# One mixed encoder layer on one core: the first head's keys move beside the gates' stage, and a weight unit's two parts share a tile

## Chip, core, metric

The kernel runs on one core of a Trainium2 chip. Its time is the device time of one execution in microseconds (us); the number quoted is the median of several runs. The profile is one further execution, recorded by the hardware profiler. The engines are named as in the profile: PE (matrix multiply; PEld its weight loads), DVE (vector), ACT (scalar), POOL, and SP, which here only issues DMAs.

## What is computed

One layer of an encoder, applied to a prompt of 1024 tokens and a sample of 2048, each with 16 learned meta tokens in front; width 1024, all in float32.

```python
xn = _rmsnorm(h, g_pre)
proj = xn @ w_in + b_in
na_q, na_k, na_v, na_z, ml_qk, ml_v, ml_z, ml_o, ml_g, mg = jnp.split(proj, SPLIT_IDX, axis=-1)
ya = (neighbourhood_attention(na_q, na_k, na_v, na_rpb) * silu(na_z)) @ w_a
yb = (mlstm(ml_qk, ml_v, ml_g, ml_o, ...) * silu(ml_z)) @ w_b
ga, gb = jnp.split(jax.nn.sigmoid(mg), 2, axis=-1)
return h + _rmsnorm((ga * ya + gb * yb) @ w_out, g_post)
```

The change touches the mLSTM branch and the weights. In the branch, queries and keys pass a convolution over three tokens and a SiLU; four heads of width 128 then run a gated linear attention in both directions, by chunks: a state per chunk from the keys and values (weighted by the gates), a scan over the states, and outputs from queries, keys, states and decay. The gates come from 16 columns of the projection, by a log-sigmoid, sums and running maxima.

## The kernel before, in words

**Precision.** Every large matmul is done with operands split in two: a high part (ACT copies with rounding) and a low part (DVE subtracts). `mm3` (L199 to L204) makes three products: high by high (L202), low by high (L203), high by low (L204). The names `whi`, `wlo` and `xh`, `xl` are such pairs.

**Two streams in one written order.** `run` (L2080) interleaves two generators. `dense` makes the projections (`group`, `sgates`) and the final stage (`final`) in the order of `PLAN`; `sparse` makes the mLSTM (`ml`) and the attention (`na`) in the order of `STEPS`: mLSTM of the prompt (s = 0), attention of it, mLSTM of the sample (s = 1), attention of it. Each `yield` of `sparse` gives a cost in us, and `dense` is advanced until it has made as much matmul work. So PE's order is written out by hand. The instructions of the other engines, and the DMA issues on SP, are put in order by a scheduler that simulates the program; each engine then works through its own list in order, and an instruction that waits holds all behind it. A tile can be written again when the last reader of its former use is done; pools that are opened later take the memory of pools that are closed.

**Weights.** `wload` (L266) loads a raw unit (128 x 1024 floats) when it is first needed; `wpump` (L277) splits it into `whi` and `wlo` (L303, L304), two tiles with four buffers each, and puts the two stores of the parts into DRAM tensors `wh` and `wl` on a list, `hold`, that `wflush` (L328, L331) empties. When the unit is needed again, two DMAs bring the parts back (L296). Units of key `"q"` are operands for a scheme with seven products in place of eight (`sgates`); there the two tiles hold two prepared operands, each with its own high and low half, loaded from the DRAM tensors `qd` (L289) and read one after the other, 12 matmuls each (L971 to L973). `wtake` hands units to the matmuls, and `wdone` frees them.

**The mLSTM.** `ml` (L1433) opens a pool `keep` for what lives through the whole sequence and, in it, a pool of scratch for `ml_gates` (L1288). That stage makes the decay factors with small matmuls (L1326 to L1394) and leaves them in `keep`. The scratch pool is closed, and a pool for the heads is opened in its place. For each head, `ml_states` (L1480) goes through the blocks of 256 tokens from the last to the first, with the 16 meta tokens as the last item: `load` brings the keys (`raw`, L1416) and the values (`va`, L1476); `conv_a` and `conv_b` make the convolution with its tanh (`cv` L1425 and L1428, `th` L1430) and the finished keys (`kf`, L1503), which are stored for later (L1505); `vsplit` weights and splits the values (`vwh` L1519, `vwl` L1520); PE transposes the keys (L1539), these are split (`kth` L1542, `ktl` L1543), and `mm3` makes the state. `raw`, `va` and `kf` have two buffers each, `cv` and `th` one. `ml_outputs` (L1574) then uses the same tiles for the queries.

**Around it.** While the prompt's mLSTM starts, `dense` is in the second group of the prompt's projections; side work (`tprep`, `wprep`, `nprep`) prepares operands of the seven-product scheme on DVE, ACT and POOL (`po`, `pr`, `xr`).

Of the kernel before, what the change touches and what calls it, by code (L numbers as in the profile page):

```python
# [137 lines left out]
class K:  # L138
# [138 lines left out]
    def wpump(self, most=NBW, parts=1, copy=None):  # L277


        nc, wp = self.nc, self.wp  # L280
        self.wload()
        while self.wraw and self.wout < most:
            key, raw, nk, w = self.wraw.popleft()
            n = nk * w
            hi = wp.tile([P, 4 * WU], F32R, name="whi", bufs=NBW)
            lo = wp.tile([P, 4 * WU], F32R, name="wlo", bufs=NBW)
            if key[0] == "q":
                for x, k in zip((hi, lo), key[1:]):
                    nc.sync.dma_start(x[:, :n].bitcast(F32), self.qd[k][:, :])  # L289
                self.wrdy.append([x[:, :n].rearrange("p (h k c) -> p h k c", h=2, k=4) for x in (hi, lo)])  # L290
                self.wout += 1
                self.wload()
                continue
            if raw is None:
                for x, d in zip((hi, lo), self.wkept[key]):
                    nc.sync.dma_start(x[:, :n].bitcast(F32), d[:, :])  # L296
            else:
                for a in range(parts):
                    c = slice(a * n // parts, (a + 1) * n // parts)
                    if copy:  # L300
                        copy(hi[:, c], raw[:, c])
                    else:
                        nc.scalar.activation(hi[:, c], raw[:, c], AF.Copy)  # L303
                    nc.vector.tensor_tensor(lo[:, c], raw[:, c], hi[:, c].bitcast(F32), op=ALU.subtract)  # L304
                if key[1] in N_COLS and key[0] == "i":
                    j = N_COLS.index(key[1])
                    for a in range(2):
                        d = self.qd[j // 2, f"{j % 2 + 1}{a + 1}"] = self.dp.tile([P, D], F32, name=f"q{j}{a}")
                        for h, x in enumerate((hi, lo)):
                            self.hold.append((d[:, 512 * h:512 * h + 512], x[:, 512 * a:512 * a + 512].bitcast(F32)))  # L310
                else:
                    self.wkept[key] = []
                for x, part in ((hi, "h"), (lo, "l")) if key in self.wkept else ():
                    d = self.dp.tile([P, n], F32, name=f"w{part}{len(self.wkept)}")
                    self.hold.append((d, x[:, :n].bitcast(F32)))
                    self.wkept[key].append(d)
                if not self.early:
                    self.wflush()
                if key[0] in "mo":
                    self.wrdy.append(None)  # L320
                    self.wout += 1
                    self.wload()
                    continue
            self.wrdy.append([x[:, :n].rearrange("p (k c) -> p k c", k=nk) for x in (hi, lo)])
            self.wout += 1
            self.wload()

    def wflush(self, most=99):  # L328
        for _ in range(min(most, len(self.hold))):
            d, x = self.hold.popleft()  # L330
            self.nc.sync.dma_start(d[:, :], x)  # L331

    def wtake(self, n):
        self.wpump()
# [1068 lines left out]
            yield A_G  # L1403
        res += out

    def conv_load(self, mp, src, c0, n, T):

        nc = self.nc
        L = NM + T
        raw = mp.tile([P, BL + 2], F32, name="raw", bufs=2)  # L1410
        a, b = max(c0 - 1, 0), min(c0 + n + 1, L)
        if a > c0 - 1:
            nc.gpsimd.memset(raw[:, 0:1], 0.0)
        if b < c0 + n + 1:
            nc.gpsimd.memset(raw[:, n + 1:n + 2], 0.0)
        nc.sync.dma_start(raw[:, a - c0 + 1:b - c0 + 1], src[:, a:b])  # L1416
        return raw

    def conv(self, mp, raw, h, is_k, n):

        nc = self.nc
        w0 = (12 if is_k else 0) + 3 * h
        w = [self.cw[:, w0 + j:w0 + j + 1] for j in range(3)]
        c = mp.tile([P, BL], F32, name="cv", bufs=1)
        nc.scalar.activation(c[:, :n], raw[:, 0:n], AF.Copy, scale=w[0])  # L1425
        yield
        for j in (1, 2):
            nc.vector.scalar_tensor_tensor(c[:, :n], raw[:, j:j + n], w[j], c[:, :n], op0=ALU.mult, op1=ALU.add)  # L1428
        th = mp.tile([P, BL], F32, name="th", bufs=1)
        nc.scalar.activation(th[:, :n], c[:, :n], AF.Tanh, scale=0.5 / (S_K if is_k else 0.5))  # L1430
        yield th, c

    def ml(self, s):  # L1433
        tc, nc = self.tc, self.nc
        T, self.seq = SEQLEN[s], s
        NB = T // BL
        with tc.tile_pool(name=f"mg{s}", bufs=1, side="right", reuse_waits="tile") as keep:
            with tc.tile_pool(name=f"mt{s}", bufs=1, side="right", reuse_waits="tile") as mp:
                self.tri = mp.tile([P, 2, P], F32, name="tri")
                nc.sync.dma_start(self.tri, self.i["tri"])  # L1440
                self.trim = keep.tile([P, 2, 1, P], F32, name="trim")
                nc.sync.dma_start(self.trim[:, :, 0, :], self.i["trimask"])
                g = []
                yield from self.ml_gates(s, keep, mp, g)
            with tc.tile_pool(name=f"ml{s}", bufs=1, side="right", reuse_waits="tile") as mp:
                self.vas = [mp.tile([P, CB, 130], F32, name=f"va{j}") for j in range(2)]
                for va in self.vas:
                    nc.gpsimd.memset(va[:, :, 128:129], 1.0)
                    nc.gpsimd.memset(va[:, :, 129:130], 0.0)
                norms = deque()  # L1450

                def step():
# [19 lines left out]
    def vload(self, mp, s, h, tok, np_, nch):  # L1472
        nc = self.nc
        va = self.vas[0]
        self.vas = self.vas[1:] + [va]
# [4 lines left out]
    def ml_states(self, mp, s, h, g, NB, sts):  # L1480

        nc = self.nc
# [4 lines left out]
        def load(i):  # L1487
            if i < N:
                n, c0 = seq[i]
                raws[i] = self.conv_load(mp, self.MK[s][h], c0, n, SEQLEN[s])  # L1490
                vas[i] = self.vload(mp, s, h, c0, min(n, P), max(1, n // P))

        def conv_a(i):
            if i < N:
                convs[i] = self.conv(mp, raws.pop(i), h, True, seq[i][0])
                next(convs[i])

        def conv_b(i):
            if i < N:
                n, c0 = seq[i]  # L1500
                th, c = next(convs.pop(i))
                kf = mp.tile([P, BL], F32, name="kf", bufs=2)
                nc.vector.scalar_tensor_tensor(kf[:, :n], th[:, :n], 1.0, c[:, :n], op0=ALU.add, op1=ALU.mult)  # L1503
                if c0:
                    nc.sync.dma_start(self.KF[s][h][:, c0 - NM:c0 - NM + n], kf[:, :n])  # L1505
# [68 lines left out]
    def ml_outputs(self, mp, s, h, g, NB, sts, norms):  # L1574
# [5 lines left out]
        def load(b):  # L1580
            if b < NB:
                t0 = b * BL
                raws[b] = self.conv_load(mp, self.MQ[s][h], NM + t0, BL, SEQLEN[s])
                kfs[b] = kf = mp.tile([P, BL], F32, name="kf", bufs=2)
# [8 lines left out]

        def vnext(b):
            if b < NB:
                vas[b] = self.vload(mp, s, h, NM + b * BL, P, CB)

        def gates(b):

# [5 lines left out]

        def conv_a(b):
            if b < NB:
                convs[b] = self.conv(mp, raws.pop(b), h, False, BL)
                next(convs[b])

        def conv_b(b):
# [51 lines left out]
        def scores(b):  # L1663
# [6 lines left out]
            s1 = mp.tile([P, CB, P], F32, name="s1", tag="th", bufs=1)  # L1670
            nc.scalar.activation(s1, s0[:, :, 1], AF.Copy)
            shs[b] = s0, s1

# [489 lines left out]
```

## Time and profile before

| what | value |
|---|---|
| median of 3 runs | 2701.97 us (2700.68 to 2704.45) |
| the profiled execution | 2708.68 us |
| its span, first to last instruction | 2706.9 us |
| PE busy | 2645.3 us |
| DVE busy | 1941.2 us |
| ACT busy | 1442.0 us |
| DMA | 805.75 MB, mean 298 GB/s |
| mean granted TensorE clock | 0.991 |

A row of a timeline gives the start in us, the length, the engine, the line of the kernel, the operation with out<-in by the program's tile names, and how many such instructions are merged (x2); in brackets stands how long the engine had been idle before it, and who ended that. Lengths of matmuls overlap, since they are pipelined. A row of the waits gives the sum in us, the number of times and the longest. A row of the table by stretches gives the length, the busy time and instructions of PE, PEld, DVE, ACT and POOL, the granted clock (1.00 is full), the busy share of the DMA engines and GB/s.

### The profile page before, as it was taken

To read this page: it belongs to the slowest core of one execution; us is meant where nothing else is said; L and a number is where in the kernel's file an instruction comes from. 1 tells how busy PE (TensorE), PEld (TensorE's weight loads), DVE (VectorE), ACT (ScalarE), POOL (GpSimd) and SP (SyncE) were. 2 spreads that over 40 slices of the span, in tenths; PEclk is the share of its full clock that TensorE was granted. 3 is DMA by queue.
4 is the path that set the end of the run, shared out by engine and by line. 5 is a ranking of instruction groups with operands and counts; after the bars stand their busy time and mean duration, and the time that the engine had idled before them with its cause. 6 is when DMAs were issued, how large, how long until landed. Compare 5 with 4: busy or idle time off the path is not lost.

```text
span 2706.9 us, 47551 instructions
## 1 busy us (share of the span) xinstructions
PE 2645.3 (98%) x15928; PEld 2334.8 (86%) x15928; DVE 1941.2 (72%) x5266; ACT 1442.0 (53%) x3388; POOL 140.0 (5%) x322
## 2 busy tenths in 40 slices
PE   9999799998989999999999999999999999999998
PEld 7998698898977999887888888888889998989888
DVE  5655588778766888545687776867478989897954
ACT  5423456545444655555665566656465665656521
POOL 0112110001000122000000000000000000000000
PEclk9999899999999999999999999999999999999999
DMA  9899887899978899888889998899899898998975
GB/s 368 339 323 341 307 307 240 297 343 339 321 231 280 296 326 313 276 265 271 253 268 328 376 296 274 274 331 362 267 312 311 264 313 270 287 301 264 317 245 208
DMA packets 402052, 805.75 MB, mean 298 GB/s; under 512 B 51632, under 2 KB 180608, under 8 KB 399504
## 3 DMA queue, kind: packets, MB, share of 16 engines
q1 hardware_dynamic: 374864, 708.79, 79.0%
q0 software_dynamic: 26944, 93.93, 9.4%
q8 instruction: 126, 2.06, 0.3%
q14 instruction: 118, 0.97, 0.1%
HBM read 548.96 MB, written 253.60 MB: 296 GB/s over the span
## 4 chain that ended last, share of the span: by engine, by line
PE 82%; DMA 10%; DVE 5%; ACT 1%; issue 1%; SPq 0%; DVEq 0%; ACTq 0%
PE pj L202 9%; PE pj L204 9%; PE pj L203 9%; PE pj L971 7%; PE pj L973 7%; PE pj L972 7%; PE pj L776 4%; PE pj L777 4%; PE pj L778 4%; PE pj L1919 3%; PE pj L1918 3%; PE pj L1920 3%; PE sm L1266 3%; PE tr L1251 2%; DMA wlo<-wl 1%
## 5 line engine op out<-in xcount | busy, mean ns | idle before, releaser
L202 PE MATMUL pj<-xh,whi 128*128 128x512 f32 (+1 forms) x896 | 345.5, 386 | 6.4 <-DMA whi<-wh 4.7
L204 PE MATMUL pj<-xh,wlo 128*128 128x512 f32 (+1 forms) x896 | 337.1, 376 | 6.5 <-DMA wlo<-wl 6.2
L203 PE MATMUL pj<-xl,whi 128*128 128x512 f32 (+1 forms) x896 | 337.6, 377 | 0.1
L776 PE MATMUL pj<-whi,xh 128*128 128x256 f32 (+1 forms) x1152 | 330.8, 287 | 6.7 <-DMA whi<-wh 5.9
L777 PE MATMUL pj<-wlo,xh 128*128 128x256 f32 (+1 forms) x1152 | 325.9, 283 | 0.7 <-DMA wlo<-wl 0.7
L778 PE MATMUL pj<-whi,xl 128*128 128x256 f32 (+1 forms) x1152 | 325.6, 283 | 0.0
L776 PEld LDWEIGHTS pj<-whi,xh 128*128 128x128 f32 x1152 | 218.1, 189 | 7.5 <-DMA whi<-wh 6.1
L1918 PE MATMUL pj<-whi,mh 128*128 128x256 f32 x768 | 219.2, 285 | 0.5 <-DMA whi<-wh 0.5
L777 PEld LDWEIGHTS pj<-wlo,xh 128*128 128x128 f32 x1152 | 217.9, 189 | 1.2 <-DMA wlo<-wl 1.0
L778 PEld LDWEIGHTS pj<-whi,xl 128*128 128x128 f32 x1152 | 218.0, 189 | 0.0
L1920 PE MATMUL pj<-whi,mlo 128*128 128x256 f32 x768 | 216.3, 282 | 0.0
L1919 PE MATMUL pj<-wlo,mh 128*128 128x256 f32 x768 | 216.2, 282 | 0.0
L204 PEld LDWEIGHTS pj<-xh,wlo 128*128 128x128 f32 x896 | 170.3, 190 | 39.8 <-DMA wlo<-wl 7.4
L202 PEld LDWEIGHTS pj<-xh,whi 128*128 128x128 f32 x896 | 170.7, 191 | 36.3 <-issue 6.3
L203 PEld LDWEIGHTS pj<-xl,whi 128*128 128x128 f32 x896 | 170.6, 190 | 27.7 <-issue 1.2
L1258 DVE TENSOR_TENSOR pts<-tr,pts 96x384 fp32r<-96x384 f32 (+2 forms) x192 | 118.5, 617 | 57.1 <-ACT pts L1253 55.2
L1253 ACT ACTIVATE pts<-tr 96x384 fp32r<-96x384 f32 (+2 forms) x192 | 103.5, 539 | 101.7 <-PE tr L1251 101.3
L202 PE MATMUL pj<-yh,whi 128*128 128x512 f32 x384 | 154.3, 402 | 0.0
L203 PE MATMUL pj<-yl,whi 128*128 128x512 f32 x384 | 151.1, 394 | 0.7 <-DVE yl L1820 0.7
L204 PE MATMUL pj<-yh,wlo 128*128 128x512 f32 x384 | 151.6, 395 | 0.0
L1918 PEld LDWEIGHTS pj<-whi,mh 128*128 128x128 f32 x768 | 145.0, 189 | 1.5 <-DMA whi<-wh 0.7
L1919 PEld LDWEIGHTS pj<-wlo,mh 128*128 128x128 f32 x768 | 145.1, 189 | 0.8
(399 smaller groups left out, 7088.1 us busy)
## 6 DMA issues: line engine op xcount, KB each, us to landing
whi<-wh SPq DMA_DIRECT2D x136, 512.0 KB
wlo<-wl SPq DMA_DIRECT2D x136, 512.0 KB
whi<-q SPq DMA_DIRECT2D x62, 512.0 KB
wlo<-q SPq DMA_DIRECT2D x50, 512.0 KB
wraw<-wu SPq DMA_DIRECT2D x48, 512.0 KB
gt<-st SPq DMA_DIRECT2D x96, 256.0 KB
tg<-gt SPq DMA_DIRECT2D x96, 256.0 KB
wh<-whi SPq DMA_DIRECT2D x36, 512.0 KB
```

The costliest lines, as they stand in the source:

```text
L202: mm(out, ah, bh, start=start, stop=False)
L203: mm(out, ah, bl, start=False, stop=False)
L204: mm(out, al, bh, start=False, stop=stop)
L776: nc.tensor.matmul(o, xh, wh, start=k == 0, stop=False)
L777: nc.tensor.matmul(o, xh, wl, start=False, stop=False)
L778: nc.tensor.matmul(o, xl, wh, start=False, stop=k == KT - 1)
L971: mm(bank, w[:, 0, k], xh[:, k], start=fresh and k == 0, stop=False, skip_group_check=True)
L972: mm(bank, w[:, 0, k], xl[:, k], start=False, stop=False, skip_group_check=True)
L973: mm(bank, w[:, 1, k], xh[:, k], start=False, stop=k == 3, skip_group_check=True)
L1918: nc.tensor.matmul(o, mh[:, k, xs], wh, start=clear > 0 and k == 0, stop=False)
L1919: nc.tensor.matmul(o, mh[:, k, xs], wl, start=False, stop=False)
L1920: nc.tensor.matmul(o, ml[:, k, xs], wh, start=False, stop=clear < 2 and k == KT - 1)
```

## The change

Two edits are made together.

1. **Keys of the first head.** The tiles `raw`, `va`, `cv`, `th` and `kf` (and `s1`, which shares a tag with `th`) move from the heads' pool to `keep`, so they don't lie in the memory of the gates' scratch. `ml_states` of head 0 is started ahead of `ml_gates`: its first step issues the loads of blocks 0 and 1. After four steps of `ml_gates` (the log-sigmoid is done, the first gate matmul is not yet written) its second step makes `conv_a(0)` and `conv_b(0)`, with the store of `kf`. The rest, from `vsplit(0)` on, comes after the gates as before, and one yield of `2 * A_D + 8.5` stands for the former two. Heads 1 to 3 do as before.
2. **One tile per weight unit.** `whi` and `wlo` become two halves of one tile `whl` with four buffers; the DRAM tensors of the two parts become one. A reload is one DMA in place of two, a store one in place of two, and the two stores per operand for `qd` become one. Units of key `"q"` are still loaded with two DMAs, one for each half.

```diff
-            hi = wp.tile([P, 4 * WU], F32R, name="whi", bufs=NBW)
-            lo = wp.tile([P, 4 * WU], F32R, name="wlo", bufs=NBW)
+            both = wp.tile([P, 2, 4 * WU], F32R, name="whl", bufs=NBW)
+            hi, lo = both[:, 0], both[:, 1]
...
             if raw is None:
-                for x, d in zip((hi, lo), self.wkept[key]):
-                    nc.sync.dma_start(x[:, :n].bitcast(F32), d[:, :])
+                nc.sync.dma_start(both[:, :, :n].bitcast(F32), self.wkept[key])
...
-                        for h, x in enumerate((hi, lo)):
-                            self.hold.append((d[:, 512 * h:512 * h + 512], x[:, 512 * a:512 * a + 512].bitcast(F32)))
+                        self.hold.append((d.rearrange("p (h c) -> p h c", h=2), both[:, :, 512 * a:512 * a + 512].bitcast(F32)))
                 else:
-                    self.wkept[key] = []
-                for x, part in ((hi, "h"), (lo, "l")) if key in self.wkept else ():
-                    d = self.dp.tile([P, n], F32, name=f"w{part}{len(self.wkept)}")
-                    self.hold.append((d, x[:, :n].bitcast(F32)))
-                    self.wkept[key].append(d)
+                    d = self.wkept[key] = self.dp.tile([P, 2, n], F32, name=f"w{len(self.wkept)}")
+                    self.hold.append((d, both[:, :, :n].bitcast(F32)))
...
-        raw = mp.tile([P, BL + 2], F32, name="raw", bufs=2)
+        raw = self.keep.tile([P, BL + 2], F32, name="raw", bufs=2)
...
-        c = mp.tile([P, BL], F32, name="cv", bufs=1)
+        c = self.keep.tile([P, BL], F32, name="cv", bufs=1)
...
-        th = mp.tile([P, BL], F32, name="th", bufs=1)
+        th = self.keep.tile([P, BL], F32, name="th", bufs=1)
...
-                g = []
-                yield from self.ml_gates(s, keep, mp, g)
-            with tc.tile_pool(name=f"ml{s}", bufs=1, side="right", reuse_waits="tile") as mp:
-                self.vas = [mp.tile([P, CB, 130], F32, name=f"va{j}") for j in range(2)]
+                self.vas = [keep.tile([P, CB, 130], F32, name=f"va{j}") for j in range(2)]
                 for va in self.vas:
                     nc.gpsimd.memset(va[:, :, 128:129], 1.0)
                     nc.gpsimd.memset(va[:, :, 129:130], 0.0)
+                g, self.keep, self.mlp, sts = [], keep, None, {}
+                states = self.ml_states(s, 0, g, NB, sts)
+                next(states)
+                for j, cost in enumerate(self.ml_gates(s, keep, mp, g)):
+                    if j == 3:
+                        next(states)
+                    yield cost
+            with tc.tile_pool(name=f"ml{s}", bufs=1, side="right", reuse_waits="tile") as mp:
+                self.mlp = mp
...
                 for h in range(4):
-                    sts = {}
-                    for cost in self.ml_states(mp, s, h, g, NB, sts):
+                    if h:
+                        sts = {}
+                        states = self.ml_states(s, h, g, NB, sts)
+                    else:
+                        yield 2 * A_D + 8.5
+                    for cost in states:
...
-                kf = mp.tile([P, BL], F32, name="kf", bufs=2)
+                kf = self.keep.tile([P, BL], F32, name="kf", bufs=2)
...
         load(0)
         load(1)
-        yield A_D + (0.0 if h else 8.5)
+        yield A_D
         conv_a(0)
-        yield A_D
+        if h:
+            yield A_D
         conv_b(0)
+        if not h:
+            yield
+            mp = self.mlp
         vsplit(0)
         yield A_D
```

More of the change, by code (lines that the diff above doesn't have):

```diff
@@ L330, in wflush @@
             d, x = self.hold.popleft()
-            self.nc.sync.dma_start(d[:, :], x)
+            self.nc.sync.dma_start(d, x)
     def wtake(self, n):
@@ L1404, in ml_gates, with conv_load @@
         res += out
-    def conv_load(self, mp, src, c0, n, T):
+    def conv_load(self, src, c0, n, T):
         nc = self.nc
         L = NM + T
-        raw = mp.tile([P, BL + 2], F32, name="raw", bufs=2)
+        raw = self.keep.tile([P, BL + 2], F32, name="raw", bufs=2)
         a, b = max(c0 - 1, 0), min(c0 + n + 1, L)
@@ L1417, in conv_load, with conv @@
         return raw
-    def conv(self, mp, raw, h, is_k, n):
+    def conv(self, raw, h, is_k, n):
         nc = self.nc
@@ L1470, in ml, with vload @@
         self.seq = None
-    def vload(self, mp, s, h, tok, np_, nch):
+    def vload(self, s, h, tok, np_, nch):
         nc = self.nc
@@ L1478, in vload, with ml_states @@
         return va
-    def ml_states(self, mp, s, h, g, NB, sts):
-        nc = self.nc
+    def ml_states(self, s, h, g, NB, sts):
+        nc, mp = self.nc, self.mlp
         seq = [(BL, NM + b * BL) for b in range(NB - 1, -1, -1)] + [(NM, 0)]
@@ L1489, in load @@
                 n, c0 = seq[i]
-                raws[i] = self.conv_load(mp, self.MK[s][h], c0, n, SEQLEN[s])
-                vas[i] = self.vload(mp, s, h, c0, min(n, P), max(1, n // P))
+                raws[i] = self.conv_load(self.MK[s][h], c0, n, SEQLEN[s])
+                vas[i] = self.vload(s, h, c0, min(n, P), max(1, n // P))
         def conv_a(i):
             if i < N:
-                convs[i] = self.conv(mp, raws.pop(i), h, True, seq[i][0])
+                convs[i] = self.conv(raws.pop(i), h, True, seq[i][0])
                 next(convs[i])
@@ L1582, in load @@
                 t0 = b * BL
-                raws[b] = self.conv_load(mp, self.MQ[s][h], NM + t0, BL, SEQLEN[s])
-                kfs[b] = kf = mp.tile([P, BL], F32, name="kf", bufs=2)
+                raws[b] = self.conv_load(self.MQ[s][h], NM + t0, BL, SEQLEN[s])
+                kfs[b] = kf = self.keep.tile([P, BL], F32, name="kf", bufs=2)
                 nc.sync.dma_start(kf, self.KF[s][h][:, t0:t0 + BL])
@@ L1595, in vnext @@
             if b < NB:
-                vas[b] = self.vload(mp, s, h, NM + b * BL, P, CB)
+                vas[b] = self.vload(s, h, NM + b * BL, P, CB)
         def gates(b):
@@ L1607, in conv_a @@
             if b < NB:
-                convs[b] = self.conv(mp, raws.pop(b), h, False, BL)
+                convs[b] = self.conv(raws.pop(b), h, False, BL)
                 next(convs[b])
@@ L1669, in scores @@
                 nc.tensor.matmul(s0[:, j, 0], kl[:, j], qh[:, j], start=False, stop=True)
-            s1 = mp.tile([P, CB, P], F32, name="s1", tag="th", bufs=1)
+            s1 = self.keep.tile([P, CB, P], F32, name="s1", tag="th", bufs=1)
             nc.scalar.activation(s1, s0[:, :, 1], AF.Copy)
```

## The prediction

> **What bounds the kernel now.** I read the page first, then the waits of PE, then PE's rows where it stood longest, then the engines in those stretches.
>
> ```profile
> span 2706.9 us, 47551 instructions
> PE 2645.3 (98%) x15928; PEld 2334.8 (86%) x15928; DVE 1941.2 (72%) x5266; ACT 1442.0 (53%) x3388; POOL 140.0 (5%) x322
> ```
>
> TensorE is the bound: 2645.3 of 2706.9 us. The change takes no matmul away, so it can only touch the 61.6 us in which PE does nothing, and what those pauses cost afterwards. The waits of PE say for whom it stands (total, times, longest):
>
> ```profile
> PE tr L1539 <- DVE kf L1503: 14.5, 2, 8.9
> PE pj L204 <- DMA wlo<-wl: 6.2, 2, 3.7
> PE pj L776 <- DMA whi<-wh: 5.9, 1, 5.9
> PE pj L202 <- DMA whi<-wh: 4.7, 1, 4.7
> ```
>
> The first row is the largest and belongs to the start of the first mLSTM head: transposes of the convolved keys `kf` (L1539) wait for DVE to finish them (L1503). The other three are loads of split weights. In order of time, with the pause and its releaser in brackets:
>
> ```profile
> 307.77 0.69 PE L1539 MATMUL tr<-ident,kf 128*128 128x128 f32 x2 [8.86 <-DVE kf L1503]
> 328.88 0.69 PE L1539 MATMUL tr<-ident,kf 128*128 128x128 f32 x2 [5.65 <-DVE kf L1503]
> ...
> 638.86 0.58 PE L776 MATMUL pj<-whi,xh 128*128 128x256 f32 x1 [5.86 <-DMA whi<-wh]
> ...
> 757.08 0.77 PE L202 MATMUL pj<-xh,whi 128*128 128x512 f32 x1 [4.69 <-DMA whi<-wh]
> 761.95 0.79 PE L204 MATMUL pj<-xh,wlo 128*128 128x512 f32 x1 [3.68 <-DMA wlo<-wl]
> ...
> 818.78 0.50 PE L204 MATMUL pj<-xh,wlo 128*128 128x512 f32 x1 [2.53 <-DMA wlo<-wl]
> ```
>
> These six pauses are 31.3 us, half of all that PE loses. A pause costs more than itself. The table by stretches shows the granted clock (PEclk) behind it:
>
> ```profile
> 308.20:311.50 3.30, 3.30 (x17) 3.30 (x16) 2.09 (x5) 0.86 (x3) 0.55 (x2) 0.50 1.03 400
> 312.00:316.00 4.00, 4.00 (x36) 4.00 (x35) 1.21 (x4) 0.75 (x3) 0.00 (x0) 1.00 1.02 410
> 329.30:332.00 2.70, 2.70 (x14) 2.70 (x13) 2.51 (x5) 1.42 (x4) 1.35 (x3) 0.50 0.47 150
> 820.30:823.50 3.20, 3.20 (x8) 1.99 (x6) 0.00 (x0) 0.00 (x0) 0.00 (x0) 0.50 1.04 410
> ```
>
> For about 3.4 us after the first pause and 2.8 us after the second PE runs at half clock, though "busy". Half of that is lost: 1.7 + 1.4 = 3.1 us. So the two pauses on `kf` are worth 14.5 + 3.1 = 17.6 us.
>
> [...]
>
> **First part: the keys of head 0.** What makes `kf` late? The queue that issues loads (SP), in order of time:
>
> ```profile
> 230.90 0.41 SPq L703 DMA_DIRECT2D mk<-st  x1
> ...
> 292.28 0.32 SPq L1416 DMA_DIRECT2D raw<-mk  x1
> ...
> 319.35 0.37 SPq L1476 DMA_DIRECT2D va<-mv  x1
> 319.81 0.41 SPq L1416 DMA_DIRECT2D raw<-mk  x1
> ```
>
> Block 0 needs what the store at 230.90 wrote, but its load goes out only at 292.28: its tile lies where the gates' scratch pool lay. Then two engines work through queues that hold other work:
>
> ```profile
> 300.67 0.49 ACT L1425 ACTIVATE cv<-raw,cw 128x256 f32<-128x256 f32 x1
> 301.07 2.44 ACT L1519 ACTIVATE vwh<-va,g_wT 128x130 fp32r<-128x130 f32 x8
> ```
>
> ```profile
> 303.26 0.48 DVE L1428 SCALAR_TENSOR_TENSOR cv<-raw,cw,cv 128x256 f32<-128x256 f32 x1
> 303.66 1.14 DVE L1520 SCALAR_TENSOR_TENSOR vwl<-va,g_wT,vwh 128x130 fp32r<-128x130 f32 x4
> ...
> 305.11 1.14 DVE L1520 SCALAR_TENSOR_TENSOR vwl<-va,g_wT,vwh 128x130 fp32r<-128x130 f32 x4
> 306.17 1.21 DVE L568 TENSOR_TENSOR po<-pr,po 128x1024 fp32r<-128x1024 f32 x1
> 307.31 0.41 DVE L1503 SCALAR_TENSOR_TENSOR kf<-th,cv 128x256 f32<-128x256 f32 x1
> ```
>
> The convolution is two ACT steps (0.49, and the tanh, near the same) and three on DVE (0.48 twice and 0.41): 2.3 us of work that took from 300.67 to 307.7, since weights' and values' splits stand between.
>
> After the change the tiles `raw`, `va`, `cv`, `th`, `kf` lie in the pool that the gates' results live in, beside the scratch, not on it. Four loads (two of keys, two of values) and the memsets on POOL are traced before the gates; the five steps of block 0 and the store of its `kf` before the gates' first matmul. The yields of this stage sum to the same, so PE's written order is unchanged. The cover for the moved steps:
>
> ```profile
> 265.00:282.00 17.00, 16.89 (x81) 11.87 (x80) 11.40 (x43) 8.82 (x20) 5.03 (x14) 1.00 0.71 261
> ```
>
> ```profile
> 265.19 0.53 PE L1326 MATMUL sm<-g_lf,tri 128*128 128x36 f32 x4
> ```
>
> From the store at 230.90 to the gates' matmuls at 265.19 lie 34 us. Estimate: the store lands in about 7 us, the load takes as much again (a wlo load below takes 7.2 us), so `raw` is in by about 246. In the gates' own 17 us DVE is free for 5.6 and ACT for 8.2; 1.4 us on DVE and about 0.9 us on ACT fit. I cost the moved steps at nothing. If that cover failed, they would stand in front of the gates' chain in the two queues, for the 2.3 us of the work itself, or for a load's 7.2 us (rival three). On SP the moved loads pass weight stores and token loads; four issues of 0.3 to 0.4 us each are 1.5 us on a queue that PE does not wait for there.
>
> What is late next? Without the first pause PE is at the transposes at 307.77 - 8.86 = 298.9. The value split (vwh, vwl) is still traced after the gates. In the trace the first state matmuls came 6.4 us behind the transposes:
>
> ```profile
> 314.15 0.28 PE L202 MATMUL sm<-vwh,kth 128*128 128x260 f32 x1
> ```
>
> At full clock that is 6.4 - 1.7 = 4.7 us, so they would be asked for at 303.6, while both splits of the values ended at 306.2. Bounds: 0 if ACT and DVE do them while the gates end (their inputs are then there), 2.6 us if they stay where they are. I take the middle, 1.3 us.
>
> The second pause, for block 2, hangs on the loads at 319.35 and 319.81. They wait for a free `va` and `raw` buffer, hence for block 0's split and convolution, and for their turn on SP. With block 0 convolved some 40 us earlier, `raw` is free before the gates end, and `va` as soon as the values are split. I count the whole pause as gone; what stands against it is rival one. First part: -17.6 + 1.3 = **-16.3 us**. For the second sequence the same edit may take away a small wait near 1270; bounds 0 and, like the first head's pauses with their clock, a few us; I take 0.
>
> **Second part: one tile and one tensor per unit.** Loads of kept weights, their stores, and the stores of operands for the products become one DMA in place of two. The two largest groups that vanish (issue times in ns: least, median, most):
>
> ```profile
> L296 SPq DMA_DIRECT2D wlo<-wl x144: 319/330/1892, 465.8 to 2675.3; - x144
> ...
> L331 SPq DMA_DIRECT2D wl<-wlo x40: 319/404/1330, 27.5 to 1004.3; - x40
> ```
>
> That is 184 issues and 144 x 0.33 + 40 x 0.40 = 64 us on SP, spread over 2700 us; bytes are the same. SP is not the bound, so this alone is worth nothing; it counts where the second part of a pair stood behind other issues:
>
> ```profile
> 751.18 0.44 SPq L296 DMA_DIRECT2D whi<-wh  x1
> ...
> 754.75 0.59 SPq L296 DMA_DIRECT2D wlo<-wl  x1
> ...
> 815.03 0.32 SPq L296 DMA_DIRECT2D whi<-wh  x1
> 816.24 0.32 SPq L296 DMA_DIRECT2D wlo<-wl  x1
> ```
>
> At 757, whi was 5.9 us under way and wlo 7.2 us (754.75 to 761.95). One DMA issued at 751.18 with twice the bytes lands, as an estimate, 0.52 MB at 300 GB/s = 1.75 us after whi did: 758.8, in place of 761.95. Against the two products that PE did in between (about 0.5 us) that saves some 2.6 us. At 818 the gap is 1.21 us, less than the 1.75 us that the longer transfer adds, so I count nothing. At 638 the same kind of pair, nothing either. On the other side each tight pair can lose 1.75 us. Bounds: a gain of 16.8 us if the four weight pauses vanished, a loss of 1.75 us at each load that is just in time today; I take **-3 us**, by the row at 757.
>
> [...]
>
> **Sum.** -16.3 - 3 = -19.3 us on the profiled execution, which took 2708.68 us with its span of 2706.9. The median of the runs is 2701.97; a stall is as long in either, so the forecast is 2701.97 - 19.3 = 2683 us.
>
> **Rivals.**
>
> One: the second pause takes the place of the first. If the loads of block 2 stay at 319 on SP, PE reaches its transposes at 328.88 - 5.65 - 8.86 - 1.7 = 312.7 and still waits until 328.9. For it: those loads came behind weight stores, and the order on SP is laid out by a scheduler ahead of time. Against: buffers are freed far earlier. Only the merge is left: 2702 - 3 = 2699 us.
>
> Two, on the other side: the pair lands as one. A unit's first product now waits for both parts; and where two prepared operands share a tile, the first can't be reloaded until the second has been read, one operand's 12 matmuls later:
>
> ```profile
> 254.88 0.23 PE pj L202
> ```
>
> ```profile
> 1957.93 0.33 SPq L289 DMA_DIRECT2D whi<-q12s  x1
> ```
>
> ```profile
> 1973.22 0.48 PE L971 MATMUL pj<-xh,whi 128*128 128x512 f32 x1
> ```
>
> 12 x 0.23 = 2.8 us later. The load at 1957.93 is first read at 1973.22, 15.3 us on, among the shortest leads of that stage; 12.5 would be left against flights of 6 to 7 us. That speaks against it. A late unit costs 1.75 us plus half clock (1.7 us): 3.5 us. It decides from 7 such units on (24.7 us, the gain and 0.2% more); 10 of them give 2683 + 35 = 2718 us.
>
> Three: the moved convolution does not fit its cover, stands before the gates' chain and holds PE at 265 for a load's 7.2 us, with the clock's 1.7: 2683 + 9 = 2692 us. The change then moves a pause more than it removes it. Against: 34 us of cover.
>
> **How the numbers follow.** Forecast 0.57, rival one 0.18, two 0.18, three 0.07. About 0.2% (5.4 us) is what a measurement of this kernel tells from no change. Faster by more than that (below 2696.6): the forecast, rival three and 0.04 of rival one, 0.68. Within: the rest of rival one, 0.14. Slower: 0.18. The range goes from 2666 (nothing late next and the weight pauses gone as well: 2702 - 17.6 - 16.8 = 2667.6, and some of their half clock) to 2708 (rival one with a few late units) and leaves out rival two. The forecast's own range is 2666 to 2694.
>
> **What would show it.** Right: no pause of PE at L1539 in the first head; `raw<-mk` issued before the gates' matmuls; half clock gone between 299 and 332; gates at the same place. The pair at 757 with one pause in place of two. Wrong: a pause at L1539 for block 2 as long as both now (rival one); new pauses of PE on the merged tile in many places (rival two); a pause at L1326 or behind it (rival three). All engines' orders are laid out anew, so pauses elsewhere may come and go; if these add more than the 19 us, the forecast fails for a reason that no row here shows.

## The result and the profile after

The changed kernel takes 2699.53 us (median of 20 runs, 2695.07 to 2704.11) against 2703.52 us for the kernel before in the same series: ratio 0.9984, 95% interval 0.9977 to 0.9991. It is faster, by 4.3 us, where 19 were forecast. Two further series gave 0.9979 [0.9970, 0.9988] and 0.9984 [0.9975, 0.9994], on the average -4.8 us. Ratios are turned into us below by 2703.

The profiled executions mislead if they are read by themselves: before's (2708.68 us) lay 5 us above its median, after's (2695.33 us) 4 us below its own. So the two traces differ by 13.4 us, the kernels by 4.8. Places and mechanisms are read from traces here, sizes from the series.

The page of after, first lines:

```profile
span 2693.5 us, 47059 instructions
PE 2642.1 (98%) x15928; PEld 2332.7 (87%) x15928; DVE 1942.3 (72%) x5266; ACT 1437.7 (53%) x3388; POOL 139.5 (5%) x322
```

492 instructions are gone, none of them PE's. The start of head 0 in after, from the timeline: the queue of loads (SP), then PE.

```profile
230.82 0.32 SPq L698 DMA_DIRECT2D mk<-st  x1
...
234.94 1.66 SPq L1411 DMA_DIRECT2D raw<-mk  x2
...
250.25 1.19 SPq L1510 DMA_DIRECT2D kf<-kf  x1
```

```profile
300.51 0.38 PE L1548 MATMUL tr<-ident,kf 128*128 128x128 f32 x2
305.11 0.28 PE L202 MATMUL sm<-vwh,kth 128*128 128x260 f32 x1
```

The keys are loaded 57 us earlier (234.94, before 292.28), and both pauses of PE on `kf` are gone: no bracket stands behind the transposes at 300.51. The stretch 290 to 340 us by itself (PE busy and its matmuls, then the other engines, granted clock, DMA share, GB/s), first before, then after:

```profile
290.00:340.00 50.00, 35.49 (x243) 34.02 (x242) 27.89 (x78) 25.46 (x61) 5.29 (x18) 0.83 0.91 320
```

```profile
290.00:340.00 50.00, 50.00 (x325) 45.34 (x324) 34.65 (x88) 29.06 (x69) 3.81 (x15) 1.00 1.00 354
```

PE loses nothing there in place of 14.5, and the granted clock is 1.00 in place of 0.83. What was gained is given back later. The waits of PE in after, and the places in order of time:

```profile
PE pj L202 <- DMA whl<-w: 8.2, 3, 3.5
PE pj L771 <- DMA whl<-w: 7.4, 2, 6.9
PE sm L204 <- DVE ktl L1552: 6.8, 3, 3.2
```

```profile
441.03 0.39 PE L204 MATMUL sm<-vwh,ktl 128*128 128x260 f32 x1 [3.25 <-DVE ktl L1552]
464.10 0.50 PE L202 MATMUL pj<-xh,whl 128*128 128x512 f32 x1 [1.65 <-DMA whl<-w]
629.88 0.58 PE L771 MATMUL pj<-whl,xh 128*128 128x256 f32 x1 [6.93 <-DMA whl<-w]
747.90 0.47 PE L202 MATMUL pj<-xh,whl 128*128 128x512 f32 x1 [3.05 <-DMA whl<-w]
803.98 0.47 PE L202 MATMUL pj<-xh,whl 128*128 128x512 f32 x1 [3.53 <-DMA whl<-w]
```

The largest wait is now that for the merged tile `whl`: 15.6 us, nearly all between 464 and 804 us. The same matmuls of ones (L370, before L375) run at 419.96 in after and at 435.88 in before, 15.9 us apart. The matmul at 747.90 ran at 757.08 in before: 9.2 us of the 15.9 are left. Whether the merge or the keys' edit did that, a single trace can't say.

### The profile page after: what moved, and what is told of

It reads as the page before. It is cut to its first block, busy times and chain, and to the rows that moved or that the text cites. A ratio compares the mean times of both kernels' runs of the same rounds, so it can differ in the third digit from the quotient of the medians.

```text
span 2693.5 us, 47059 instructions
## 1 busy us (share of the span) xinstructions
PE 2642.1 (98%) x15928; PEld 2332.7 (87%) x15928; DVE 1942.3 (72%) x5266; ACT 1437.7 (53%) x3388; POOL 139.5 (5%) x322
## 4 chain that ended last, share of the span: by engine, by line
PE 79%; DMA 11%; DVE 6%; ACT 2%; issue 1%; SPq 0%; POOL 0%; DVEq 0%; ACTq 0%; POOLq 0%
PE pj L202 8%; PE pj L204 8%; PE pj L203 8%; PE pj L966 7%; PE pj L968 7%; PE pj L967 7%; PE pj L771 4%; PE pj L773 4%; PE pj L772 4%; PE pj L1928 3%; PE pj L1927 3%; PE pj L1929 3%; DMA whl<-w 3%; PE sm L1261 3%; PE tr L1246 2%
## 5 line engine op out<-in xcount | busy, mean ns | idle before, releaser
L202 PE MATMUL pj<-xh,whl 128*128 128x512 f32 (+1 forms) x960 | 369.6, 385 | 9.8 <-DMA whl<-w 8.2
L204 PE MATMUL pj<-xh,whl 128*128 128x512 f32 (+1 forms) x960 | 362.0, 377 | 0.3 <-DVE whl L303 0.3
L203 PE MATMUL pj<-xl,whl 128*128 128x512 f32 (+1 forms) x960 | 360.7, 376 | 0.1
L771 PE MATMUL pj<-whl,xh 128*128 128x256 f32 (+1 forms) x1152 | 331.4, 288 | 8.1 <-DMA whl<-w 7.4
L773 PE MATMUL pj<-whl,xl 128*128 128x256 f32 (+1 forms) x1152 | 327.3, 284 | 0.0
L772 PE MATMUL pj<-whl,xh 128*128 128x256 f32 (+1 forms) x1152 | 326.9, 284 | 0.0
L771 PEld LDWEIGHTS pj<-whl,xh 128*128 128x128 f32 x1152 | 219.2, 190 | 9.2 <-DMA whl<-w 7.8
L772 PEld LDWEIGHTS pj<-whl,xh 128*128 128x128 f32 x1152 | 219.1, 190 | 0.2
L1927 PE MATMUL pj<-whl,mh 128*128 128x256 f32 x768 | 218.3, 284 | 0.9 <-DMA whl<-w 0.9
L773 PEld LDWEIGHTS pj<-whl,xl 128*128 128x128 f32 x1152 | 219.1, 190 | 0.0
L202 PEld LDWEIGHTS pj<-xh,whl 128*128 128x128 f32 x960 | 181.4, 189 | 42.5 <-issue 8.3
L1928 PE MATMUL pj<-whl,mh 128*128 128x256 f32 x768 | 216.3, 282 | 0.0
L1929 PE MATMUL pj<-whl,mlo 128*128 128x256 f32 x768 | 215.5, 281 | 0.0
L204 PEld LDWEIGHTS pj<-xh,whl 128*128 128x128 f32 x960 | 181.4, 189 | 35.5 <-DVE whl L303 0.5
L966 PE MATMUL pj<-xh,whl 128*128 128x512 f32 x512 | 206.7, 404 | 1.1 <-ACT pj L983 1.1
L968 PE MATMUL pj<-xh,whl 128*128 128x512 f32 x512 | 202.0, 395 | 0.0
```

What stands on the lines that cost most here:

```text
L202: mm(out, ah, bh, start=start, stop=False)
L203: mm(out, ah, bl, start=False, stop=False)
L204: mm(out, al, bh, start=False, stop=stop)
L771: nc.tensor.matmul(o, xh, wh, start=k == 0, stop=False)
L772: nc.tensor.matmul(o, xh, wl, start=False, stop=False)
L773: nc.tensor.matmul(o, xl, wh, start=False, stop=k == KT - 1)
```

## The experiments

The theory from here on, **M**: the keys' edit brings what was forecast and the merge takes most of it back. Its rivals: **P**, the profiled execution of before had longer pauses than its usual ones, so the keys' edit has less to win; **O**, every engine's order is laid out anew and the scatter of that is the whole difference.

**Each part alone.** `e1_keys` keeps two tiles, two tensors and two DMAs per unit and moves only the keys; `e2_merge` is the kernel before with `whl` alone:

```
e1:  hi = wp.tile([P, 4 * WU], F32R, name="whi", bufs=NBW)   # as before
     lo = wp.tile([P, 4 * WU], F32R, name="wlo", bufs=NBW)
     ...
e2:  both = wp.tile([P, 2, 4 * WU], F32R, name="whl", bufs=NBW)
     ...
     nc.sync.dma_start(both[:, :, :n].bitcast(F32), self.wkept[key])
```

Beside them ran the two kernels themselves once more.

> Only the first edit: head 0's keys beside the gates; weight units stay two tiles. Theory M (the merge takes back what the keys give): 14 to 18 us faster than before, no pause at the first head's transposes. Theory P (the profiled execution of before had longer pauses than its usual ones): 3 to 6 us faster. Theory O (every order is laid out anew and the pauses of PE move elsewhere): anything from 10 us faster to 5 slower, with the pauses at the first head gone and new ones of as much in the groups behind it.

> Only the second edit: one tile and one tensor per weight unit; keys as before. Theory M: 10 to 14 us slower than before. Theory P: within 3 us of before. Theory O: the pauses at the first head's transposes stay (about 14 us in the profile), the other pauses are drawn anew, and the time lies within 8 us of before on either side.

> The kernel before, unchanged, for a second profile. All theories: ratio 1.000 within 0.1%. Theory P: the two pauses at L1539 are together under 8 us in this profile, in place of 14.5. Theories M and O: 13 to 16 us again.

> The changed kernel, unchanged, for a second profile. All theories: 3 to 5 us faster than before. Theory P: its pauses of PE differ from those of the first profile by 5 us and more in sum. Theories M and O: the same pauses at the same places, within 2 us each.

Measured: the keys alone 2689.77 us, ratio 0.9942 [0.9929, 0.9954], -15.7 us; the merge alone 2711.58 us, 1.0020 [1.0010, 1.0030], +5.4 us; before again 1.0009 [1.0000, 1.0018], after again 0.9979. In a later series the keys alone gave 0.9928 [0.9914, 0.9941], -19.5 us; the mean of both is -17.6. So M holds for the keys (it expected 14 to 18 us) and in its direction for the merge: beside the keys that costs 17.6 - 4.8 = 12.8 us by these means, by itself 5.4, where M had expected 10 to 14. The 12.8 is uncertain by some 3 us, since the means go over several series, and the median of before itself moves between 2702.95 and 2707.88 us from one to the other. In the one series that held both, the changed kernel lies 9 to 10 us above the keys alone (medians 2698.95 and 2689.77, ratios 0.9979 and 0.9942). P falls: the keys alone bring their gain, and the second profile of before has 13.5 us of pauses on `kf`. The merge alone, where PE waits in it:

```profile
303.21 0.44 PE L1534 MATMUL tr<-ident,kf 128*128 128x128 f32 x2 [2.52 <-DVE kf L1498]
320.16 0.69 PE L1534 MATMUL tr<-ident,kf 128*128 128x128 f32 x2 [3.18 <-DVE kf L1498]
...
469.50 0.54 PE L202 MATMUL pj<-xh,whl 128*128 128x512 f32 x1 [2.41 <-DMA whl<-w]
602.36 0.39 PE L771 MATMUL pj<-whl,xh 128*128 128x264 f32 x1 [1.07 <-DMA whl<-w]
...
756.02 0.77 PE L202 MATMUL pj<-xh,whl 128*128 128x512 f32 x1 [6.00 <-DMA whl<-w]
817.18 0.77 PE L202 MATMUL pj<-xh,whl 128*128 128x512 f32 x1 [6.87 <-DMA whl<-w]
```

At 756 one pause of 6.00 stands where 4.69 + 3.68 = 8.37 stood before: a gain of 2.4, as the prediction had it. At 817 6.87 us stand for 2.53, and at 469 and 602 pauses are new: +4.3 + 2.4 + 1.1, on weights +5.4 in sum. That this is also the time measured is chance: the pauses on `kf` fell from 14.5 to 5.7 us here (the keys' load goes out at 286.04, 6 us sooner than in before). So the merge costs some 5.4 + 8.8 = 14 us behind them, about as much as beside the keys' edit.

In all the traces PE runs the same matmuls in the same order, so the start of one and the same matmul can be compared between kernels. By that, e2 is 8.3 us ahead of before at 440 us and 3.7 us behind it at the end: 12 us are lost. At the pause of 469 us it loses 4.3, at that of 817 4.6, both with half clock behind the pause (0.55 and 0.50), and 3.6 at a pause of 1.91 us on DVE (`yg`, at 916.13), where before has none; gains and losses elsewhere nearly cancel.

**What in the merge costs.** Three readings: **W**, the pair lands as one, so a product waits for twice the bytes; **S**, the merged store can start only when the low part is split, and the slot is reloaded only after it; **T**, one tile is one buffer, freed when both parts are done with, whatever DMAs move it. O stays in play. Each kernel is the changed one with some DMAs cut in two:

```
x1:  for h in range(2):                        # reload: two halves of the columns
         c = slice(h * n // 2, (h + 1) * n // 2)
         nc.sync.dma_start(both[:, :, c]..., self.wkept[key][:, :, c])
x2:  for x, h in zip((hi, lo), range(2)):      # reload: by part
         nc.sync.dma_start(x[:, :n]..., self.wkept[key][:, h])
x3:  for h in range(2):                        # store: by part
         self.hold.append((d[:, h], both[:, h, :n]...))
                                               # the operands' stores for qd likewise
x5:  x2 and x3 together                        # only tile and tensor are merged
y7:  x1 and x3 together
```

> The changed kernel, but each kept unit is loaded again by two DMAs, one for each half of its columns with both parts; tile, tensor and store stay merged. So far: keys alone 2689.8, whole change 2699.5, so the merge costs about 10 us beside the keys' edit. Theory W (the pair lands as one: the first product waits for twice the bytes of one long transfer): the first half lands as early as the first part did, the weight pauses shrink to those of the keys alone, 2688 to 2692. Theory S (the merged store starts only when the low part is split, so the reload goes out later): the reload is issued at the same time as in the changed kernel, 2696 to 2700. Theory T (one tile holds both parts and comes free only when both have been read and stored): 2697 to 2702, weight pauses as now. Theory O (the laid out order scatters by several us whatever is edited): any of 2690 to 2705, with pauses at other places.

> The changed kernel, but each kept unit is loaded again by two DMAs, one for each part as before the change; tile, tensor and store stay merged. Theory W: 2688 to 2692, as the keys alone, since a product waits for its own part only. Theory S: about 2697 to 2700, the reloads behind the late stores are still late. Theory T: 2697 to 2702, the weight pauses of 420 to 830 us stay near 20 us in sum. Theory O: any of 2690 to 2705.

> The changed kernel, but a split unit is stored by two DMAs, one for each part as before the change; tile, tensor and reload stay merged. Theory W: no change, 2697 to 2701, the reload still lands as one. Theory S: the high part's store starts ahead of the low part's split, the slot is free earlier, 2690 to 2693. Theory T: 2697 to 2702. Theory O: any of 2690 to 2705.

> The changed kernel with loads and stores by part, all DMAs as before the change; only the tile and the tensor are one for both parts. Theories W and S, each or both: 2688 to 2692, as the keys alone. Theory T: the tile alone makes the loss, 2697 to 2702 with the weight pauses of the changed kernel. Theory O: any of 2690 to 2705, with pauses at other places than the changed kernel's.

Then, on one chip with the keys alone:

> The keys' edit alone once more, now on one chip beside the three kernels below: 2688 to 2692 (first time 2689.8, ratio 0.994), pauses on weights' loads between 400 and 930 us near 8 us in sum. It is the mark for what the merge adds.

> Keys' edit with one tile and one tensor per unit, but all its DMAs by part (first time 2692.3, ratio 0.995, beside another series of runs than the keys alone). Theory T (one tile frees both parts together, so the first part's reload goes out at the second part's time): 4 us or more above the keys alone, 2693 to 2697. Theories W and S (the cost lies in the merged transfers): within 2 us of the keys alone, 2688 to 2692.

> The changed kernel with its reload in two column halves and its store in two parts. If long transfers are what the merge costs (W with S): near the version with all DMAs by part, 2690 to 2693. If the halves add nothing to the stores by part: 2692 to 2696. Theory T: 2694 to 2698.

and, to part the reload from the store within one series:

> The changed kernel once more, beside the three below on one chip: ratio 0.998 as before, pauses on weights' loads of 15 to 17 us between 400 and 930 us. It is the mark for the next two.

> Merged store, reload by part. If the merged reload is the larger cost: 4 to 8 us below the changed kernel of this series. If the merged store is: 0 to 3 us below it (the first series gave 1.6 us).

> Merged reload, store by part. If the merged store is the larger cost: 4 to 8 us below the changed kernel of this series (the first series gave 7 us). If the merged reload is: 0 to 3 us below it; its pauses on weights' loads were not shorter, which speaks for this.

| kernel | ratio to before [95%] | us, by 2703 |
|---|---|---|
| changed kernel, three series | 0.9984 [0.9977, 0.9991], 0.9979 [0.9970, 0.9988], 0.9984 [0.9975, 0.9994] | -4.8 mean |
| x2, reload by part | 0.9973 [0.9962, 0.9983], 0.9981 [0.9969, 0.9992] | -7.3, -5.1 |
| x1, reload by halves | 0.9964 [0.9952, 0.9976] | -9.7 |
| x3, store by part | 0.9956 [0.9941, 0.9971], 0.9965 [0.9953, 0.9977] | -11.9, -9.5 |
| x5, both by part | 0.9950 [0.9933, 0.9967], 0.9940 [0.9926, 0.9954] | -13.5, -16.2 |
| y7, halves and store by part | 0.9934 [0.9921, 0.9948] | -17.8 |
| e1, keys alone | 0.9942 [0.9929, 0.9954], 0.9928 [0.9914, 0.9941] | -15.7, -19.5 |

By their times x1, x2 and x3 of the first series (2696.64, 2697.91 and 2692.57 us) lie where S had put them; W by itself had put x1 and x2 at 2688 to 2692. That series held no changed kernel. In the last one, which did, the medians were 2700.18 (changed), 2697.45 (x2) and 2696.14 us (x3). T falls as the main cause: with all DMAs by part the merged tile is 2.2 and 3.2 us behind the keys alone, and the intervals overlap; a rest of that size for the tile is not excluded. Its mechanism is there: in x5's second run the two parts of the unit read at 799 us are issued together (787.03, two in a row), with the keys alone beside it at 783.82 and 787.46. Of W and S neither does it alone. The store by part brings 6 us (-10.7 against -4.8), the reload by part 1.4 (by halves 5, in one series), both by part 10, and y7 is as fast as the keys alone within the noise. These differences too go across series. Where each acts shows in the queue of loads; first the keys alone, then the changed kernel, then x3:

```profile
442.81 0.33 SPq L331 DMA_DIRECT2D wh<-whi  x1
447.29 0.41 SPq L331 DMA_DIRECT2D wl<-wlo  x1
449.76 0.32 SPq L296 DMA_DIRECT2D whi<-wh  x1
```

```profile
446.33 0.54 SPq L326 DMA_DIRECT2D w<-whl  x1
456.79 1.27 SPq L295 DMA_DIRECT2D whl<-w  x2
```

```profile
438.02 0.33 SPq L328 DMA_DIRECT2D w<-whl  x1
446.05 0.77 SPq L328 DMA_DIRECT2D w<-whl  x1
454.27 0.60 SPq L295 DMA_DIRECT2D whl<-w  x1
```

With two stores the high part is on its way before the low part is split, at 438 to 443 us, and reloads begin at 449.76 or 454.27. The merged store waits until 446.33 (in after ACT is done with the high part at 439.52, DVE with the low part at 444.53), and the first reload behind it goes out at 456.79. That is the new pause at 464 (1.65 us; 3.79 in the third run of the changed kernel, 0.96 in that of x3, none with the keys alone). At the other three the merged reload itself goes out late, as the section on the prediction shows. In the last series, x2 and x3:

```profile
PE pj L772 <- DMA whl<-w: 6.6, 1, 6.6
PE pj L202 <- DMA whl<-w: 4.5, 1, 4.5
```

```profile
PE pj L202 <- DMA whl<-w: 12.5, 3, 7.7
PE pj L773 <- DMA whl<-w: 8.8, 2, 8.1
```

With the reload by part the waits sum to 13.1 us between 400 and 930 us (these two and 2.0 on the low parts), with the reload merged to 21.3, in spite of the better time (x2's trace is its slowest run, 8 us above its median). By place: of the same matmuls, x3 starts that of 419.82 in the third run of the changed kernel 1.5 us sooner (418.36), that of 603.75 6.4 us sooner (597.32), and that of 822.37 only 4.0 us sooner (818.39). So the store by part wins in the stretch of the late store, and behind it the merged reload still loses. How W and S share the cost is settled only roughly, because the waits on DVE and ACT in the same stretch differ as well: 12.7 us in x2 and 7.1 in x3. Of this, 3.6 us are waits on `st` that x3 doesn't have; the rest includes `ktl` (longest 3.25 against 2.65 us) and `yg` (1.91 against 1.05). They come with another order on these engines. O has that much: a few us, not the whole.

**Half the bytes.** To see whether landing itself is what PE waits for, the reload brings the high part alone:

```
nc.sync.dma_start(hi[:, :n].bitcast(F32), self.wkept[key][:, 0])
lo = hi
```

> The changed kernel, but a kept unit's reload brings the high part alone, half the bytes, and the products of the low part read the high part: the low parts are left out of the result, every instruction of PE stays. If the landing of the long transfer is the cause (W): the pauses on weights' loads between 400 and 930 us fall from 15 to 17 us to under 5, the time to 2680 to 2688. If the late start of the reload is (T or S): each pause loses at most the 2 us that half the bytes save, 8 to 10 us stay, 2690 to 2695.

Measured 2682.96 us, 0.9906 [0.9892, 0.9921]. Its waits between 400 and 930 us:

```profile
PE sm L204 <- DVE ktl L1553: 6.0, 4, 3.2
PE sm L202 <- ACT kth L1552: 5.9, 2, 5.3
PE pj L202 <- DMA whl<-w: 2.3, 1, 2.3
```

The waits on weights fall to 2.3 us, from 15.6 in the first trace of the changed kernel (17.1 and 19.2 in the other two). The one that stays is the one at 465 us, behind the merged store. So the waits hang on the bytes of the reload, as W says; S or T by itself would have left 8 to 10 us. Whether the single pair's landing does it or the relief of the DMA engines (from 720 to 930 us busy 0.68 at 228 GB/s, in after 0.80 at 273) can't be told apart here, since the bytes of all kept units were halved.

**Smaller still.** The keys alone, with each part reloaded in two column halves:

```
for h in range(2):
    c = slice(h * n // 2, (h + 1) * n // 2)
    for x, d in zip((hi, lo), self.wkept[key]):
        nc.sync.dma_start(x[:, c].bitcast(F32), d[:, c])
```

> The keys' edit alone, two tiles as before, but each part is loaded again in two column halves: four transfers per unit in place of two. If the size of a transfer matters in itself while the DMA engines are full, the step that cost about 10 us one way brings some the other way: 2683 to 2687. If it costs only because a product waits for bytes that it does not need yet and halves are needed almost at once: 2687 to 2691. If more issues on SP are a price: 2690 to 2695.

Measured 2688.25 us, 0.9938 [0.9921, 0.9955]: the same as the keys alone. So neither the transfer's size nor the number of issues shows a price of its own here, within the interval of 4.6 us on either side. The stretch 600 to 930 us, for after (1 MB per reload), the keys alone (512 KB) and this kernel (256 KB):

```profile
600.00:930.00 330.00, 311.35 (x1992) 282.53 (x1993) 239.95 (x632) 163.22 (x360) 34.57 (x66) 0.97 0.86 299
```

```profile
600.00:930.00 330.00, 316.99 (x2073) 287.87 (x2072) 247.01 (x647) 167.76 (x369) 35.74 (x68) 0.99 0.88 305
```

```profile
600.00:930.00 330.00, 319.98 (x2085) 291.62 (x2084) 248.59 (x651) 170.37 (x373) 37.80 (x72) 0.98 0.89 309
```

The DMA engines move 299, 305 and 309 GB/s; the larger transfers are not faster.

The best version is the keys' edit without the merge: 2689.77 and 2688.96 us, below both kernels.

## Why the prediction was wrong

- **The keys' pauses (-17.6): right.** Both are gone with their half clock, the cover for the moved steps held (the `kf` store is out at 250.25, ahead of the gates), and the part alone measured -15.7 and -19.5 against -16.3.
- **Late next (1.3): wrong place.** Where it was placed, nothing is late: the first state matmul follows the transposes after 4.6 us (300.51, 305.11) without a pause. Other pauses grew instead. Waits of the keys alone between 400 and 930 us:

```profile
PE sm L204 <- DVE ktl L1557: 5.0, 6, 1.7
PE pj L776 <- DMA whi<-wh: 4.6, 1, 4.6
PE pj L204 <- DMA wlo<-wl: 2.7, 2, 1.5
PE sm L202 <- ACT kth L1556: 2.6, 1, 2.6
PE pj L375 <- ACT st L367: 2.2, 1, 2.2
PE pj L777 <- DMA wlo<-wl: 0.8, 1, 0.8
```

- The waits on DVE and ACT are 10 us there (with one of 0.6), 3.4 in before (`ktl` 2.5, `stT` 0.9); those on weights fell from 17.5 (6.2 + 5.9 + 4.7 + 0.7) to 8.1. The forecast had neither, and they nearly cancel. That the first part came out so close is in part that luck.
- **The merge (-3): the step that failed.** The prediction put it as "One DMA issued at 751.18 with twice the bytes lands, as an estimate, [...] 1.75 us after whi did", and for the other two places "I count nothing". By itself the pair at 757 did what was said. But its pause was the exception: with the keys moved, only 1.24 us of it were left to gain. The rows of the keys alone that stand for after's last three:

```profile
625.99 0.58 PE L776 MATMUL pj<-whi,xh 128*128 128x256 f32 x1 [4.59 <-DMA whi<-wh]
627.36 0.58 PE L777 MATMUL pj<-wlo,xh 128*128 128x256 f32 x1 [0.78 <-DMA wlo<-wl]
...
744.36 0.50 PE L204 MATMUL pj<-xh,wlo 128*128 128x512 f32 x1 [1.24 <-DMA wlo<-wl]
...
798.48 0.50 PE L204 MATMUL pj<-xh,wlo 128*128 128x512 f32 x1 [1.50 <-DMA wlo<-wl]
```

- Against them after has 6.93 for 5.37, 3.05 for 1.24, 3.53 for 1.50, and 1.65 at 464 for nothing: four units, 1.6 to 2.0 us each, 7 us. By the starts of the same matmuls, which take in the half clock behind some of these pauses, after falls back by 1.9 (464), 1.4 (630), 1.8 (748) and 3.6 us (804), 8.7 in all. This is rival two's mechanism at 1.4 to 3.6 us per late unit, where the rival put 3.5, with four units where the sum had none and the rival's threshold was seven.
- **Not all of it is weights.** Another 3.7 us are lost at a pause on DVE, the matmul that the keys alone start at 893.13 without one:

```profile
902.69 0.37 PE L1214 MATMUL sm<-kd,stk 128*128 128x288 f32 x1 [1.91 <-DVE yg L1276]
```

- In after DVE runs a step on `kx` (901.29, 0.94 us) ahead of the `yg` that PE waits for; with the keys alone it comes behind it (893.47). Every kernel with `whl` has this pause, 1.9 us or, in x3, 1.05. It is the kind that the prediction named and didn't price ("pauses elsewhere may come and go").
- **And the merged DMA was not issued at the first part's time.** Issue times of the reloads behind the four pauses:

| PE starts on it in after | keys alone: high part | keys alone: low part | after: the pair |
|---|---|---|---|
| 464.10 | 449.76 | 453.22 | 456.79 |
| 629.88 | 612.43 | 614.20 | 621.05 |
| 747.90 | 734.67 | 738.28 | 739.89 |
| 803.98 | 780.83 | 785.91 | 789.83 |

- PE itself is 0.9 us ahead of the keys alone at the first of these and 1.6, 2.2 and 4.0 behind at the others; with that taken off, the pair goes out at the second part's time (the last two) or some 5 us behind it (the first two). Why SP is that late at 621.05 is not shown. The third in the queue of loads, first the keys alone, then after:

```profile
734.67 0.45 SPq L296 DMA_DIRECT2D whi<-wh  x1
...
738.28 0.47 SPq L296 DMA_DIRECT2D wlo<-wl  x1
```

```profile
739.89 0.56 SPq L295 DMA_DIRECT2D whl<-w  x1
```

- It goes out at about the second part's time (739.89; PE was ready for the unit at 747.90 - 3.05 = 744.85, with the keys alone for its second product at 743.1) and lands 8.0 us later, at 747.90. Its flight was estimated well (5.9 + 1.75 = 7.7); its start was not. The flight isn't the same everywhere: the pair issued at 789.83 is read 14.2 us later. For the tile that waits for a store, the merged store puts the start later again, which the sum did not have.
- **A wrong row at 818.** For the pause there the prediction took the pair issued at 815.03 and 816.24, 1.21 us apart. Counted on from the unit of 757 us, the load that PE waits for at 818.78 is the fourth after it; its parts went out at 800.40 and 805.02, 4.6 us apart, and the second was under way for 13.8 us. So the reason given for counting nothing there doesn't hold.
- **The rivals.** One: both pauses are gone, so it did not happen. Two: as above; the product at 747.90, which reads the high part alone, starts 8.0 us behind the issue of the pair, where it was 5.9 us for that part by itself in before (751.18 to 757.08). Its other half, the operands' reload 2.8 us later, shows nothing, for no wait of PE on operands stands among after's waits. Three: no pause of that size at the gates.

## What to carry to other kernels

Merging two DMAs saves issues, and their number on SP showed no price here (each part reloaded by two DMAs in place of one: 2688.25 us, against 2689.77 and 2688.96, with 4.6 us of interval on either side). It ties the first part's start and end to the second's, in the reload and in the store; here four units lost 1.4 to 3.6 us each, by the starts of the same matmuls. Count it not at the pair with the widest gap (2.4 us gained at 757 in the merge alone) but at every pair that is just in time, and add the store in front: here the merged one went out at 446.33, the high part's by itself at 438.02. Where a stage's loads are already late, give the consumer the part that it needs first as a transfer of its own: with reload and store by part the kernel lay at -13.5 and -16.2 us here, merged at -4.8.

## What was not expected of the hardware

The same pause costs a half clock in one kernel's execution and none in another's. Behind the pause of 3.25 us on `ktl`, in after and in x1:

```profile
442.50:445.90 3.40, 3.40 (x12) 2.83 (x11) 2.37 (x5) 2.11 (x4) 0.00 (x0) 0.50 0.78 302
```

```profile
442.10:445.50 3.40, 3.40 (x19) 2.83 (x18) 2.42 (x6) 2.46 (x6) 0.00 (x0) 1.00 0.87 307
```

12 matmuls against 19 in the same 3.4 us. In x2 (first run) the half clock behind this pause lasts nearly twice as long:

```profile
442.40:449.00 6.60, 6.57 (x22) 5.56 (x23) 5.48 (x11) 5.06 (x11) 0.00 (x0) 0.56 0.82 300
```

Twenty matmuls behind the pause PE is 3.55 us on in x1 (440.56 to 444.11), 5.15 in after and 6.24 in x2. What decides whether the half clock comes, stays away or lasts longer behind the same pause is not shown. It stands behind shorter pauses too: in before behind the 2.53 us that end at 818.78 (0.50 from 820.30 to 823.50), in after behind the 1.91 us on `yg` (0.59 in the 3.4 us from 902.69). The rows may also bear on the spread of one kernel's runs (9 us for the changed one): the mean granted clock was 0.991 in the profiled execution of before, 0.995 in after's and 0.997 with the keys alone, and the half clock behind a pause is best priced here as a range, 0 to 2.7 us (3.55 against 6.24).
